# Pinning every weight fetch of a decoder block to the program's order on its queue

## The chip, the cores and the metric

The kernel runs on one core of one Trainium2 chip. The metric is the time of one execution on the device, in microseconds (us). The core has five engines that run side by side: TensorE (PE in the profile; PEld is its weight load), VectorE (DVE), ScalarE (ACT), GpSimd (POOL) and SyncE (SP). Here SP does nothing but issue transfers from HBM into the on-chip memory SBUF. It takes its instructions strictly one after the other: an issue whose buffer isn't free yet holds up all issues behind it.

## The reference

One decoder block of width 2048 over 256 tokens, all in float32. Cut to what matters here:

```python
def reference(x, mix_norm_w, w_in, ..., w_out, ffn_norm_w, w_gate_up, w_down, final_norm_w):
    h = x
    h = h + hybrid_mixer(rmsnorm(h, mix_norm_w), w_in, ..., w_out)
    h = h + swiglu(rmsnorm(h, ffn_norm_w), w_gate_up, w_down)
    return rmsnorm(h, final_norm_w)

def hybrid_mixer(h, w_in, ..., w_out):
    proj = einsum('bsd,de->bse', h, w_in)
    (q, k, v, g_out, gk_low, gate_b, gate_c, xc, merge_a, merge_b) = split(proj)
    y_a = rmsnorm(gla_chunked(q, k, v, log_g)) * silu(g_out)
    y_b = gate_b * causal_depthwise_conv(gate_c * xc, conv_w)
    merged = sigmoid(merge_a) * y_a + sigmoid(merge_b) * y_b
    return einsum('bse,ed->bsd', merged, w_out)

def swiglu(h, w_gate_up, w_down):
    gate, up = split(einsum('bsd,df->bsf', h, w_gate_up))
    return einsum('bsf,fd->bsd', silu(gate) * up, w_down)
```

Nearly all the work is the four large products with `w_in`, `w_out`, `w_gate_up` and `w_down`, and all of their weights are read from HBM once.

## The kernel before, in words

**Pieces.** The host lays every weight matrix out in pieces of 128 x 1024 floats, 512 KB each: two blocks of 128 rows by 512 columns (for k and q four by 256, for the last two strips of `w_down` four by 256). A list written out ahead (`stream_list`, made of `piece_list`, `gates_list`, `hidden_list` and `down_list`) says in which order the pieces are multiplied: first k, q and v with the linear attention, then the gates of the mixer, `w_out`, the hidden layer of the feed-forward part mixed with `w_down`, and the rest of `w_down`.

**What happens to a piece.** SP fetches it into a tile `raw` (5 buffers). ACT rounds it into a tile `hi` (`high`, L238; 6 buffers), DVE takes the rest, `raw - hi`, into a tile `lo` (`low`, L243; 5 buffers). PE then does three products for each pair of blocks (`mm3`, L347 to L349: lo, hi, hi), for plain pieces ("eights") for both halves of the tokens, 12 matmuls in all.

**Block sums.** Twelve pairs of 512-column strips (the four gc/xc pairs of the gates, as `GATES` names them, and eight fg/fu pairs of the hidden layer) are multiplied by a scheme with seven block products in place of eight (`sevens`, L398). For each of four quarters q of the depth it uses the pieces "11", "t1", "t3", "t2", "t4" and for the lower blocks "21" and "22" (`seven_list`, L100). Each has 6 matmuls. The four "t" pieces are sums of weight blocks, made by DVE when the piece is loaded (`sum_of`, L245):

- "11" fetches its block into the tile `y` (1 buffer) and uses it as it is.
- "t1" fetches another block into the tile `x` (2 buffers) and writes `raw = y + x` (L259).
- "t3" fetches a third block into `raw` and adds it into `x` (L265); "t2" adds `y` into `x` (L265); "t4" fetches a fourth block into `raw` and adds it into `x` (L265). "t3", "t2" and "t4" are all rounded out of the same tile `x`.

So each quarter makes four fetches: y, x, raw, raw. The tile `y` comes free once "t2" is summed; the two tiles `x` take turns.

**Mixing.** `mixed` (L107) sets plain pieces between the pieces of a pair: at most one behind each "t" piece first, then behind "21" and "22" (in one gate pair, where `early` is set, behind "11" too). In the hidden layer a pair but the first (which `FIRST` spaces by itself) gets 15 or 16 plain pieces, which lie behind the "t" pieces, so that the last eight pieces of a pair, 21 and 22, follow each other with nothing between; this is called the tail of the pair below.

**The order of the fetches.** `take` (L335) loads pieces in the list's order, up to five ahead of the one in use, by `load_piece` (L268). Plain pieces are fetched at L295 in `load_piece`, all blocks for the sums at L232 in `fetch`. Both are issues on SP's queue. The program's order on that queue is the order in which these lines are run. The order in which the engine in fact gets them is fixed when the program is built, by a scheduler that puts an instruction forward when its inputs and buffers are ready sooner. `pin` (`tc.keep_in_program_order`, L187) binds one instruction behind the one that the program traced just before it on the same engine; it adds no wait and no instruction. In the kernel before, some DVE and ACT instructions are pinned, and no transfer is.

**Other transfers on SP.** The start's loads of x, half of the stores at the end, and one quarter of the second reading of x into the tile `h` (`read_h`, L1000 to L1007), which comes after the mixer, in the middle of `w_out`: it is run seven pieces behind the gates' last (L1009), and `h` lies in memory that the gates' work tiles held before. The other three quarters of it go through POOL's queue.

Of the kernel before, what the change touches and what calls it, by code (L numbers as in the profile page):

```python
# [184 lines left out]
def block_kernel(ctx, tc, x, xt, cols_in, gkw_in, gku_in, gnw, conv_w, finw, w_in, w_out, w_gu, w_dn, out):  # L185
    nc = tc.nc
    pin = tc.keep_in_program_order  # L187
    mats = {"w_in": w_in, "w_out": w_out, "w_gu": w_gu, "w_dn": w_dn}
# [40 lines left out]
    def fetch(key, k0, pool=wraw, tag="raw"):  # L229
        mat, j, n, w = index[(key, k0)]  # L230
        raw = pool.tile([P, n, w], F32, tag=tag, name=tag, bufs={"x": 2, "y": 1}.get(tag))
        nc.sync.dma_start(raw, mats[mat][j].rearrange("p (k c) -> p k c", c=w))  # L232
        return raw

    def high(raw, piece, a=0, b=None):
        hi, n = piece[0], piece[2]
        ks = slice(a, b or n)
        nc.scalar.copy(hi[:, ks, :], raw[:, ks, :])  # L238

    def low(raw, piece, a=0, b=None):  # L240
        hi, lo, n = piece
        ks = slice(a, b or n)
        nc.vector.tensor_tensor(out=lo[:, ks, :], in0=raw[:, ks, :], in1=hi[:, ks, :].bitcast(F32), op=ALU.subtract)  # L243

    def sum_of(pair, what, q):  # L245

        one, two = pair
        if what == "21":
            return fetch(one, 4 * q + 2)
        if what == "22":  # L250
            return fetch(two, 4 * q + 2)
        if what == "11":
            held["y"] = fetch(one, 4 * q, held["pool"], "y")
            return held["y"]
        y = held["y"]
        if what == "t1":
            held["x"] = fetch(two, 4 * q, held["pool"], "x")
            raw = wraw.tile([P, 2, 512], F32, tag="raw", name="raw")
            nc.vector.tensor_tensor(out=raw, in0=y, in1=held["x"], op=ALU.add)  # L259
            return raw  # L260
        x = held["x"]
        if halfway and halfway[-1][0] is x:
            finish_low()
        other = y if what == "t2" else fetch(two if what == "t3" else one, 4 * q + 2)
        nc.vector.tensor_tensor(out=x, in0=x, in1=other, op=ALU.add)  # L265
        return x

    def load_piece():  # L268


        i = count["loaded"]
        count["loaded"] += 1
        if i < len(stream):
            key, k0 = stream[i]
            if isinstance(k0, tuple):
                n, w = 2, 512
                raw = sum_of(key, *k0)
                step = n
            else:
                mat, j, n, w = index[(key, k0)]  # L280
                raw = wraw.tile([P, n, w], F32, tag="raw", name="raw")

                step = n // 2 if i < 2 else n
            piece = [whi.tile([P, n, w], F32R, tag="hi", name="hi"), None, n]
            if isinstance(k0, tuple):
                high(raw, piece)
                halfway.append((raw, piece, key, k0))
            else:
                if i < 2:
                    piece[1] = wlo.tile([P, n, w], F32R, tag="lo", name="lo")  # L290
                for a in range(0, n, step):
                    b = a + step
                    if (i, a) in hooks:
                        hooks.pop((i, a))()
                    nc.sync.dma_start(  # L295
                        raw[:, a:b, :], mats[mat][j, :, a * w:b * w].rearrange("p (k c) -> p k c", c=w))
                    high(raw, piece, a, b)
                    if i < 2:
                        low(raw, piece, a, b)
                if i < 2:  # L300
                    ready[(key, k0)] = piece
                else:
                    halfway.append((raw, piece, key, k0))
        if len(halfway) > 1 or (halfway and i >= len(stream)):
            finish_low()

    def finish_low():
        raw, piece, key, k0 = halfway.pop(0)
        piece[1] = wlo.tile([P, piece[2], PIECE // piece[2]], F32R, tag="lo", name="lo")
        low(raw, piece)  # L310
        ready[(key, k0)] = piece
# [23 lines left out]
    def take(key, k0):  # L335
        while count["loaded"] <= len(stream) and count["loaded"] <= count["used"] + LOOK:
            load_piece()
        return ready.pop((key, k0))
# [902 lines left out]
```

## Time and profile before

| what | value |
|---|---|
| median of 3 runs | 1505.6 us (1505.35, 1505.6, 2092.2) |
| the profiled execution's own time | 1504.81 us |
| its span, first to last instruction | 1503.1 us |
| TensorE clock granted | 0.999 |
| ACT busy | 864.1 us, 57% |
| read from HBM | 351.03 MB |
| transfers, mean over the span | 239 GB/s, the fastest fortieth 349 GB/s |
| weight fetches issued by SP | 650: 362 at L295, 288 at L232 (192 into raw, 48 into x, 48 into y) |

The page counts the time that an engine is busy and, ahead of each group of instructions, the time that it sat idle and what ended that. For a transfer it gives the time of issue on SP's queue and the time from there to landing. A step of the kernel is late only if PE has to wait for it, so the rows to look at are PE's waits; everything ahead of PE has some lead over it.

### The profile page before, as it was taken

The numbers are of one execution on the slowest core, as the hardware profiler recorded it, in microseconds if no ns is written. First come the engines' busy times: TensorE is split into PE (matmuls) and PEld (weight loads), VectorE is DVE, ScalarE is ACT, GpSimd is POOL, SyncE is SP. The second block draws the span as 40 slices with busy tenths as digits, with TensorE's granted clock in tenths as the row PEclk, the third lists the DMA queues.
The fourth block names the chain that finished last, engine by engine and source line by source line (L and its number), as shares of the span: only waits on it lengthen the run. The fifth ranks groups of instructions, "written<-read, shape, count | busy, mean of one in ns | idle before, by whom it ended". The sixth has DMA issues, their size and how long they took to land.

```text
span 1503.1 us, 19370 instructions
## 1 busy us (share of the span) xinstructions
PE 1489.7 (99%) x7064; PEld 1244.8 (83%) x7064; DVE 1277.8 (85%) x1283; ACT 864.1 (57%) x977; POOL 38.0 (3%) x60
## 2 busy tenths in 40 slices
PE   9999999999999999999999999999999999999997
PEld 8989988888887888888888888888888788888887
DVE  6785868979979878966689999999999999999975
ACT  7773546655655655654566755655565556565553
POOL 0030000000000000000000000000000000000000
PEclk9999999999999999999999999999999999999999
DMA  9656557876876878787677777776877788787782
GB/s 349 201 172 174 177 166 251 288 225 234 285 259 232 297 237 257 249 258 215 209 221 219 238 253 251 250 253 218 275 242 239 259 255 277 242 264 234 231 297 90
DMA packets 100128, 358.58 MB, mean 239 GB/s; under 512 B 11492, under 2 KB 11620, under 8 KB 99904
## 3 DMA queue, kind: packets, MB, share of 16 engines
q1 hardware_dynamic: 96656, 346.73, 70.8%
q0 software_dynamic: 2800, 8.89, 2.2%
q10 hardware_dynamic: 576, 1.72, 0.3%
q8 instruction: 55, 0.90, 0.2%
q14 instruction: 41, 0.34, 0.1%
HBM read 351.03 MB, written 2.10 MB: 235 GB/s over the span
## 4 chain that ended last, share of the span: by engine, by line
PE 53%; DVE 1%; issue 0%; ACT 0%; DVEq 0%; ACTq 0%
PE fg L347 8%; PE fg L349 8%; PE fg L348 8%; PE dn L347 5%; PE dn L349 5%; PE dn L348 5%; PE wo L347 2%; PE wo L348 2%; PE wo L349 2%; PE fu L349 1%; PE fu L347 1%; PE fu L348 1%; PE trb L595 1%; PE mb L349 0%; PE mb L348 0%
## 5 line engine op out<-in xcount | busy, mean ns | idle before, releaser
L243 DVE TENSOR_TENSOR lo<-raw,hi 128x1024 fp32r<-128x1024 f32 (+1 forms) x506 | 612.0, 1217 | 110.9 <-ACT hi L238 27.9
L238 ACT CAST hi<-raw 128x1024 fp32r<-128x1024 f32 (+1 forms) x506 | 523.9, 1047 | 269.9 <-PE gb L349 27.7
L238 ACT CAST hi<-x 128x1024 fp32r<-128x1024 f32 x144 | 151.7, 1053 | 267.4 <-DVE x L265 207.1
L243 DVE TENSOR_TENSOR lo<-x,hi 128x1024 fp32r<-128x1024 f32 x144 | 176.1, 1223 | 37.5 <-ACT hi L238 26.6
L347 PE MATMUL dn<-lo,acth 128*128 128x512 f32 (+1 forms) x368 | 140.7, 382 | 1.7 <-DVE h L1098 0.9
L349 PE MATMUL dn<-hi,acth 128*128 128x512 f32 (+1 forms) x368 | 139.9, 380 | 0.0
L348 PE MATMUL dn<-hi,actl 128*128 128x512 f32 (+1 forms) x368 | 139.9, 380 | 0.0
L265 DVE TENSOR_TENSOR x<-x,raw 128x1024 f32<-128x1024 f32 x96 | 117.0, 1218 | 12.0 <-DMA raw<-in_w_in_dram 7.7
L347 PE MATMUL fg<-lo,hh 128*128 128x512 f32 x288 | 112.4, 390 | 0.0
L349 PE MATMUL fg<-hi,hh 128*128 128x512 f32 x288 | 112.2, 390 | 0.0
L348 PE MATMUL fg<-hi,hl 128*128 128x512 f32 x288 | 112.2, 389 | 0.0
L347 PE MATMUL fg<-lo,sh 128*128 128x512 f32 x256 | 101.0, 395 | 0.0
L348 PE MATMUL fg<-hi,sl 128*128 128x512 f32 x256 | 99.9, 390 | 0.0
L349 PE MATMUL fg<-hi,sh 128*128 128x512 f32 x256 | 99.8, 390 | 0.0
L347 PEld LDWEIGHTS dn<-lo,acth 128*128 128x128 f32 x368 | 69.2, 188 | 15.8 <-DVE h L1098 1.8
L349 PEld LDWEIGHTS dn<-hi,acth 128*128 128x128 f32 x368 | 69.2, 188 | 13.3
L348 PEld LDWEIGHTS dn<-hi,actl 128*128 128x128 f32 x368 | 69.2, 188 | 12.9
L347 PEld LDWEIGHTS fg<-lo,hh 128*128 128x128 f32 x288 | 54.1, 188 | 11.8 <-DVE lo L243 0.5
L349 PEld LDWEIGHTS fg<-hi,hh 128*128 128x128 f32 x288 | 54.1, 188 | 11.3
L348 PEld LDWEIGHTS fg<-hi,hl 128*128 128x128 f32 x288 | 54.1, 188 | 11.0
L243 DVE TENSOR_TENSOR lo<-y,hi 128x1024 fp32r<-128x1024 f32 x48 | 58.5, 1218 | 4.8 <-ACT hi L238 2.1
L259 DVE TENSOR_TENSOR raw<-y,x 128x1024 f32<-128x1024 f32 x48 | 58.5, 1219 | 4.2 <-DMA y<-in_w_in_dram 3.3
(247 smaller groups left out, 3070.1 us busy)
## 6 DMA issues: line engine op xcount, KB each, us to landing
raw<-in_w_in_dram SPq DMA_DIRECT2D x254, 512.0 KB, 4.5
raw<-in_w_gu_dram SPq DMA_DIRECT2D x176, 512.0 KB, 4.4
raw<-in_w_dn_dram SPq DMA_DIRECT2D x88, 512.0 KB, 4.5
x<-in_w_gu_dram SPq DMA_DIRECT2D x32, 512.0 KB, 4.8
y<-in_w_gu_dram SPq DMA_DIRECT2D x32, 512.0 KB, 3.9
raw<-in_w_out_dram SPq DMA_DIRECT2D x32, 512.0 KB, 4.3
y<-in_w_in_dram SPq DMA_DIRECT2D x16, 512.0 KB, 4.4
x<-in_w_in_dram SPq DMA_DIRECT2D x16, 512.0 KB, 4.8
```

What stands on the lines that cost most here:

```text
L238: nc.scalar.copy(hi[:, ks, :], raw[:, ks, :])
L243: nc.vector.tensor_tensor(out=lo[:, ks, :], in0=raw[:, ks, :], in1=hi[:, ks, :].bitcast(F32), op=ALU.subtract)
L259: nc.vector.tensor_tensor(out=raw, in0=y, in1=held["x"], op=ALU.add)
L265: nc.vector.tensor_tensor(out=x, in0=x, in1=other, op=ALU.add)
L347: nc.tensor.matmul(ps, lhsT=sh, rhs=ml, start=first, stop=False, skip_group_check=onto)
L348: nc.tensor.matmul(ps, lhsT=sl, rhs=mh, start=False, stop=False, skip_group_check=onto)
L349: nc.tensor.matmul(ps, lhsT=sh, rhs=mh, start=False, stop=last, skip_group_check=onto)
L595: nc.tensor.transpose(out=ps[:, j, :], in_=src[:, j * P:(j + 1) * P], identity=ident)
```

## The change

Both lines that fetch weights wrap their issue in `pin`. Nothing else is changed: the same transfers, the same buffers, the same lists.

```diff
     def fetch(key, k0, pool=wraw, tag="raw"):
         mat, j, n, w = index[(key, k0)]
         raw = pool.tile([P, n, w], F32, tag=tag, name=tag, bufs={"x": 2, "y": 1}.get(tag))
-        nc.sync.dma_start(raw, mats[mat][j].rearrange("p (k c) -> p k c", c=w))
+        pin(nc.sync.dma_start(raw, mats[mat][j].rearrange("p (k c) -> p k c", c=w)))
         return raw
...
                     if (i, a) in hooks:
                         hooks.pop((i, a))()
-                    nc.sync.dma_start(
-                        raw[:, a:b, :], mats[mat][j, :, a * w:b * w].rearrange("p (k c) -> p k c", c=w))
+                    pin(nc.sync.dma_start(
+                        raw[:, a:b, :], mats[mat][j, :, a * w:b * w].rearrange("p (k c) -> p k c", c=w)))
                     high(raw, piece, a, b)
```

Each weight fetch is thereby bound behind whatever the program traced on SP just before it, a weight fetch or one of the other transfers.

## The prediction, made before the changed kernel ran

> **What bounds the kernel now.** I read the page's first lines, then the waits of TensorE (PE), then windows.
>
> ```profile
> span 1503.1 us, 19370 instructions
> PE 1489.7 (99%) x7064; PEld 1244.8 (83%) x7064; DVE 1277.8 (85%) x1283; ACT 864.1 (57%) x977; POOL 38.0 (3%) x60
> ```
>
> PE is busy for 1489.7 of 1503.1 us. All that it waited for, added up over the whole run, is this (us in total, times, longest):
>
> ```profile
> PE warm_ps L518 <- DVE spare L514: 1.3, 1, 1.3
> PE dn L347 <- DVE h L1098: 0.9, 2, 0.5
> PE trb L595 <- DVE sb L908: 0.9, 1, 0.9
> PE dn L347 <- DVE lo L243: 0.8, 1, 0.8
> PE g L347 <- DVE lo L243: 0.7, 1, 0.7
> PE gc L347 <- DVE lo L243: 0.5, 1, 0.5
> PE gb L347 <- DVE ya L919: 0.2, 1, 0.2
> PE k L348 <- DVE lo L243: 0.2, 1, 0.2
> ```
>
> The first and the last of these belong to the start, which the change leaves alone. The other six make 4.0 us, and only three of them, 0.8 + 0.7 + 0.5 = 2.0 us, are waits for a weight piece that came late. So PE sets the time, and no order of the fetches can win more than these few us. What it can do is to lose: in the hidden layer DVE is nearly as full as PE. The next windows are a stretch of the gates with about two pairs and two single pairs of the hidden layer (columns: length, busy time of PE, PEld, DVE, ACT, POOL, clock, share of the DMA engines, GB/s).
>
> ```profile
> 400.00:640.00 240.00, 238.39 (x1058) 196.51 (x1057) 211.62 (x197) 138.02 (x143) 9.94 (x18) 1.00 0.79 257
> 860.00:942.00 82.00, 82.00 (x371) 67.94 (x370) 76.50 (x73) 49.63 (x54) 0.00 (x0) 1.00 0.76 246
> 1109.00:1190.00 81.00, 80.51 (x359) 66.16 (x358) 76.32 (x73) 45.33 (x48) 0.00 (x0) 1.00 0.77 253
> ```
>
> In the last window DVE has 81.0 - 76.3 = 4.7 us to spare in one pair, in the gates 240.0 - 211.6 = 28.4 in two. That is the cover for anything that the change makes late on DVE.
>
> One rule speaks against the bound. The Trainium skill, Perfetto Trace Analysis, section Identifying the Most-Contended Engine, says that the busy share of matmuls is no measure of the distance to the limit, and that the busy share of the weight loads is. By it, 83% here, 1503.1 - 1244.8 = 258 us would be in hand. The window from 860 to 942 us disagrees: PE waits for nothing in it, 82.00 of 82.00, and the weight loads are at 67.94, 83%, so 83% is what full pace looks like in this kernel.
>
> **What the change moves.** It adds no instruction, no transfer and no wait. It only forbids the order that the issues have now. This is SP's queue around one pair, from the tail of the pair before (1080 us) to the third quarter of the next:
>
> ```profile
> 1080.54 0.42 SPq L232 DMA_DIRECT2D x<-in_w_gu_dram  x1
> ...
> 1083.63 2.75 SPq L232 DMA_DIRECT2D raw<-in_w_gu_dram  x2
> 1087.19 0.33 SPq L232 DMA_DIRECT2D y<-in_w_gu_dram  x1
> 1090.72 1.47 SPq L232 DMA_DIRECT2D raw<-in_w_gu_dram  x2
> 1094.26 0.33 SPq L232 DMA_DIRECT2D x<-in_w_gu_dram  x1
> 1095.39 6.16 SPq L232 DMA_DIRECT2D raw<-in_w_gu_dram  x4
> ...
> 1119.94 0.33 SPq L232 DMA_DIRECT2D y<-in_w_gu_dram  x1
> ...
> 1132.57 0.42 SPq L232 DMA_DIRECT2D x<-in_w_gu_dram  x1
> 1136.88 0.33 SPq L232 DMA_DIRECT2D y<-in_w_gu_dram  x1
> ```
>
> The code has y, then x, in each quarter ("11" stands just ahead of "t1"). The trace has them otherwise: the first two x and the first y of the pair are fetched between the eight raw fetches of the tail before, and the third x goes out ahead of its y. The raw fetches among themselves are already in the code's order. So the change moves addends, x nearly always and y at the start of a pair, to a later place. There are 12 pairs, each with one start and three inner quarters.
>
> *Inner quarters.* y goes out when it does now, since its one buffer comes free with the sum of "t2", and x follows at once behind it. What that costs is how much later than y the x lands. The start of the first pair, the one place with y and x back to back in the code's order, tells it; then come the landings in the hidden layer (y first, then x) and the three sums of the pair above:
>
> ```profile
> L232 SPq DMA_DIRECT2D y<-in_w_in_dram x1: 327/327/327, 212.1 to 212.1; - x1
> DMA to landing us min/median/max: 3.6/3.6/3.6
> ...
> L232 SPq DMA_DIRECT2D x<-in_w_in_dram x2: 425/428/432, 212.5 to 212.9; - x2
> DMA to landing us min/median/max: 4.5/5.3/6.0
> ```
>
> ```profile
> DMA to landing us min/median/max: 3.3/3.9/5.0
> ...
> DMA to landing us min/median/max: 4.2/5.9/7.0
> ```
>
> ```profile
> 1108.73 1.22 DVE L259 TENSOR_TENSOR raw<-y,x 128x1024 f32<-128x1024 f32 x1
> 1125.27 1.21 DVE L259 TENSOR_TENSOR raw<-y,x 128x1024 f32<-128x1024 f32 x1
> 1141.46 1.22 DVE L259 TENSOR_TENSOR raw<-y,x 128x1024 f32<-128x1024 f32 x1
> ```
>
> At the start y lands at 212.1 + 3.6 = 215.7 and the first x at 212.5 + 4.5 = 217.0, 1.3 us behind it. Second quarter: y, issued at 1119.9, lands by the median at 1123.8, x would at 1125.1, and the sum begins at 1125.27: nothing lost. Third: y at 1136.9 + 3.9 = 1140.8, x at 1142.1, the sum begins at 1141.46: 0.6 us late. The fourth I take like the third. That makes 1.2 us per pair on DVE. The early x bought little, as its landing shows: 5.9 us in the middle against 3.9 for y, since it was put behind a queue that was already full.
>
> PE sees this only where it has no lead left. In most pairs the 4.7 us swallow the 1.2; in the three places where PE already waits for a piece I let all of it through: 3 x 1.2 = **+3.6 us**. Bounds: 0, if the lead holds everywhere, and 12 x 1.2 = 14.4, if it holds nowhere.
>
> *The tails.* Three transfers leave the tail of each pair, where raw lands slowly (issues between 1095 and 1102 us):
>
> ```profile
> DMA to landing us min/median/max: 4.1/4.9/5.7
> ```
>
> The fastest landing in the hidden layer is 3.3 and one transfer displaces the next by 1.3, so the pieces there can come about 1 us sooner, which is enough to end the three waits for late pieces: **-2.0 us**. Bounds: 0, and -4.0, if all six waits go.
>
> *The starts of pairs.* y and x are now issued behind the tail's last raw, at the earliest at 1095.39 + 6.16 = 1101.6. y lands by 1106.6 (5.0, the slowest), x 1.3 later at 1107.9, and the sum begins at 1108.73. I cost it at **0**; the raw fetches ahead hide it, 0.8 us remain, and with the slowest x (7.0) it would be 1102.0 + 7.0 - 1108.7 = 0.3 us, 3 us in 12 pairs.
>
> *The reading of h.* SP's share of it is traced ahead of the 13th and 14th pieces of `w_out` (counted in the lists), and stands behind them now, because it waits for the last transposes of the mixer:
>
> ```profile
> 717.62 7.89 SPq L295 DMA_DIRECT2D raw<-in_w_out_dram  x4
> 730.73 0.38 SPq L1007 DMA_DIRECT2D h<-in_x_dram  x1
> ...
> SPq L1007 <- PE trb L595: 4.9, 1, 4.9
> ...
> L295 SPq DMA_DIRECT2D raw<-in_w_out_dram x2: 328/328/328, 722.5 to 725.2; - x2
> ...
> DMA to landing us min/median/max: 4.9/7.3/9.3
> ...
> 700.00:748.00 48.00, 33.95 (x145) 26.78 (x146) 1.38 (x2) 1.00 0.67 215
> ```
>
> Pinned, both wait for h: they go out at 731.1 and 731.5 in place of 722.5 and 725.2, up to 8.6 us later. The last row counts matmuls into wo: 145 have begun by 748.0, so the 13th piece (12 a piece) begins there. With the slowest landing of h, 9.3, and the rounding and rest of 1.05 and 1.22 us
>
> ```profile
> L238 ACT CAST hi<-x 128x1024 fp32r<-128x1024 f32 x144 | 151.7, 1053 | 267.4 <-DVE x L265 207.1
> L243 DVE TENSOR_TENSOR lo<-x,hi 128x1024 fp32r<-128x1024 f32 x144 | 176.1, 1223 | 37.5 <-ACT hi L238 26.6
> ```
>
> it is ready at 742.7. The lead on PE hides it with 5.3 us over: **0**. Behind them queue the first pair's y and x, now fetched far ahead; without the cover the place costs at most 8.6 - 5.3 = 3.3 us.
>
> **The sum.** 1504.8 (the profiled execution's own time; its span and 1.7 around it) + 3.6 - 2.0 = 1506.4. The median of the runs lies 0.8 above the profiled execution: **1507.2 us**.
>
> **Rivals.**
>
> *The tails win.* All lateness is swallowed and the six waits vanish: 1505.6 - 4.0 = 1501.6. For it: the spare 4.7 us per pair. Against it: half of these waits are for work (L1098, L908, L919) that has no weight in it.
>
> *Nothing that PE sees.* The issues change places, or hardly do, and PE's waits stay as they are: 1505.6. The rows of the queue speak against the second, the lead of PE for the first.
>
> *The lateness adds up.* The lead is used up in every pair: 1505.6 + 14.4 = 1520.0. For it: three places have no lead now. Against it: 1.2 is a quarter of 4.7.
>
> *Slower: the addend becomes DVE's clock.* If x, behind y in a full queue, takes as long as the slowest now does, 7.0 against 3.9, each inner quarter is 3.1 us late and DVE stands still in front of the sum, since all its later work is behind it. Three make 9.3 us per pair; 4.7 are covered, 4.6 go through. The gates' pairs have 14 us of room each; the first hidden pair, mixed with `w_out`, I count with them. Seven pairs make 32.2, 1537.8 us. It decides from 4.7 / 3 = 1.6 us per quarter on. Against it: the back-to-back landing, 1.3. The Trainium skill, Trainium Kernel Development and Optimization, section Best Practices, asks for two buffers so that transfers overlap with compute; x has two and would use the second later than now. By that advice this rival has it; the rows say that the second buffer's head start was mostly spent in the queue.
>
> *PE was not at its limit.* If the rule on weight loads held, a smoother supply could free up to 258 us, but nothing in this change touches the spacing of the matmuls, and without waits they stand as close as anywhere.
>
> **How the numbers follow.** Forecast 1507.2: 0.47. Nothing seen, 1505.6: 0.15. Tails win, 1501.6: 0.17. Lateness adds up, 1520.0: 0.14. Addend as clock, 1537.8: 0.06. PE not at its limit: 0.01. The range runs from 1501.4 to 1520.5, which leaves out the last two and the edges. 2% of 1505.6, 30.1 us, is about what a measurement of this kernel can tell from no change. Faster by that is only the last case, as PE's busy time alone, 1489.7, is above 1475.5: 0.01. Slower by that is the fourth rival: 0.06. The rest is within: 0.93.
>
> **What would show it.** In the queue's timeline y stands directly ahead of x in every quarter, and no x or y stands in a tail. x lands 1 to 2 us behind y, at a shorter time from issue than 5.9. DVE's waits for an addend at L259 come to some 12 x 1.2 = 14 us in all. PE's waits for lo stay under 6 us. h stands ahead of two more raw fetches of `w_out`, and PE has no wait there. I am wrong if PE's waits for lo repeat once per quarter or per pair, if PE waits near 748 us, or if the time falls under 1501.

## The result, and the profile after

The changed kernel takes 1523.2 us in the median of five runs (1520.2 to 1524.7), against 1505.6 us for the kernel before: 1.0110 times as long, 95% interval 1.0093 to 1.0128. (The ratio is that of the means, without the one slow execution of the kernel before, 2092.2 us.) By the medians that is 17.6 us more, 2.7 us above the upper end of the predicted range and 16.0 above the predicted time. The profiled execution took 1523.48 us, with a span 18.7 us longer than before.

First the page of the changed kernel, span and busy times:

```profile
span 1521.8 us, 19369 instructions
PE 1497.4 (98%) x7064; PEld 1245.5 (82%) x7064; DVE 1275.5 (84%) x1283; ACT 859.8 (56%) x977; POOL 38.0 (2%) x60
```

The work is the same; PE's busy time grew by 7.7 us (1497.4 against 1489.7), so part of the loss isn't a wait at all. PE's waits in the changed kernel (us in total, times, longest):

```profile
PE trb L595 <- DVE sg L1057: 4.6, 4, 2.0
PE fg L347 <- DVE lo L243: 3.6, 7, 0.9
PE tr L581 <- ACT hraw L584: 2.6, 1, 2.6
PE dn L347 <- DVE h L1098: 1.9, 2, 1.2
PE g L347 <- DVE lo L243: 1.4, 1, 1.4
PE warm_ps L518 <- DVE spare L514: 1.3, 1, 1.3
PE trb L595 <- issue: 0.5, 1, 0.5
PE gc L347 <- DVE lo L243: 0.5, 1, 0.5
PE k L348 <- DVE lo L243: 0.2, 1, 0.2
```

Without the start they come to 15.1 us; before they were 4.0. Waits for a late weight piece (lo) are the smaller part, 5.5 us. The larger part is for *finished work*: the transposes of a finished hidden block (`trb`, of the product `sg`) and of the normalised h (`tr`). No fetch feeds those. How a late fetch holds them up is the core of this case.

DVE's waits for an addend at L259, and the queue of SP around a tail and an inner quarter of the changed kernel:

```profile
DVE raw L259 <- DMA x<-in_w_gu_dram: 16.6, 20, 3.0
DVE raw L259 <- DMA x<-in_w_in_dram: 7.4, 4, 3.0
```

```profile
1127.93 0.33 SPq L232 DMA_DIRECT2D y<-in_w_gu_dram  x1
1128.31 0.42 SPq L232 DMA_DIRECT2D x<-in_w_gu_dram  x1
...
1176.52 16.12 SPq L232 DMA_DIRECT2D raw<-in_w_gu_dram  x8
1192.69 0.43 SPq L232 DMA_DIRECT2D y<-in_w_gu_dram  x1
1193.17 0.42 SPq L232 DMA_DIRECT2D x<-in_w_gu_dram  x1
```

The order is the one foretold: y directly ahead of x, and no addend among the eight raw fetches of the tail. The sums wait 24.0 us for x, where before it was 4.2, and nearly all of that for y. Taken row by row, 16.5 of the 24.0 us lie at inner quarters and 7.5 at starts of pairs.

**Where the time goes.** One row for each kernel splits the loss: DVE's product of a finished hidden block, with the start of its first and last instance (ns of one: min, median, max; then first and last start). Before, then after:

```profile
L1057 DVE SCALAR_TENSOR_TENSOR sg<-u,r,sg x16: 737/746/753, 857.7 to 1443.1; 128x512 f32<-128x512 f32 x16
```

```profile
L1057 DVE SCALAR_TENSOR_TENSOR sg<-u,r,sg x16: 741/752/753, 861.1 to 1461.9; 128x512 f32<-128x512 f32 x16
```

Up to the first one 3.4 us are lost (861.1 - 857.7). From there to the last the hidden layer takes 600.8 in place of 585.4 us: 15.4 us. These two numbers are read from the same row for every experiment below and called **the head** and **the hidden stretch**. They belong to the profiled execution, which lies up to 2.4 us from the median of its kernel. The gates lose nothing: SP's issue of h, which waits for the mixer's last transposes, stands at 730.00 us after and at 730.73 before. Their sums do wait for x (7.4 us), but the gates have the room.

### The profile page after: what moved, and what is told of

Its sections match the earlier page's. It is cut to its first block, busy times and chain, and to the rows that moved or that the text cites. A ratio compares the mean times of both kernels' runs of the same rounds, so it can differ in the third digit from the quotient of the medians.

```text
span 1521.8 us, 19369 instructions
## 1 busy us (share of the span) xinstructions
PE 1497.4 (98%) x7064; PEld 1245.5 (82%) x7064; DVE 1275.5 (84%) x1283; ACT 859.8 (56%) x977; POOL 38.0 (2%) x60
## 4 chain that ended last, share of the span: by engine, by line
PE 86%; DVE 6%; DMA 3%; issue 2%; ACT 2%; SPq 0%; DVEq 0%; ACTq 0%
PE fg L347 6%; PE fg L349 6%; PE fg L348 6%; PE dn L347 4%; PE dn L348 4%; PE dn L349 4%; DVE lo L243 3%; PE gc L347 3%; PE gc L348 3%; PE gc L349 3%; PE v L348 2%; PE v L347 2%; PE v L349 2%; PE gb L349 2%; PE gb L347 2%
## 5 line engine op out<-in xcount | busy, mean ns | idle before, releaser
L349 PEld LDWEIGHTS dn<-hi,acth 128*128 128x128 f32 x368 | 69.2, 188 | 13.4
L259 DVE TENSOR_TENSOR raw<-y,x 128x1024 f32<-128x1024 f32 x48 | 58.6, 1220 | 24.0 <-DMA x<-in_w_gu_dram 16.6
```

The costliest lines, as they stand in the source:

```text
L349: nc.tensor.matmul(ps, lhsT=sh, rhs=mh, start=False, stop=last, skip_group_check=onto)
```

## The experiments

Line numbers in an experiment's rows are those of its own kernel, up to eight lines further down. Each was timed beside the kernel before, in 4 to 11 executions; ratios are to that.

### Which of the pins does it

*The addends free*: plain fetches and h pinned, x and y not.

```diff
-        pin(nc.sync.dma_start(raw, mats[mat][j].rearrange("p (k c) -> p k c", c=w)))
+        load = nc.sync.dma_start(raw, mats[mat][j].rearrange("p (k c) -> p k c", c=w))
+        if tag not in ("x", "y"):
+            pin(load)
```

> The changed kernel with the addends x and y not pinned; all fetches into raw stay pinned, behind h too. Theory (the pins cost where they move the addends, and at h): only the loss at h is left, 1505.6 + 4.4 = 1510.0. Rival 1 (the addends are all of it): 1505.6. Rival 2 (the pins on raw, or the order that they give the other engines, cost by themselves): above 1514.

Measured: 1505.47 us, ratio 1.0005 (0.9996 to 1.0013); head +1.4, hidden stretch +0.5 (859.1 to 1445.0). That is the first rival's number, not the theory's: without the pins on the addends there is no loss, to within the interval's 2 us. The plain fetches pinned behind h, which stand behind it in this kernel's queue too, cost little by themselves, but not nothing: PE waits 1.5 us for `hraw` at 742 us, where it waited for nothing before, and the head is longer by about that.

*h on POOL's queue*, all weight fetches pinned:

```diff
-            (nc.gpsimd if j else nc.sync).dma_start(h[:, :, j * 512:(j + 1) * 512], xv[:, :, j * 512:(j + 1) * 512])
+            nc.gpsimd.dma_start(h[:, :, j * 512:(j + 1) * 512], xv[:, :, j * 512:(j + 1) * 512])
```

> The changed kernel with the one quarter of the reading of h that SP issues moved to POOL's queue, so that no weight fetch can stand behind it. Matched matmuls of the two traces lie 0.7 us apart just before 736 us (the changed one ahead) and 3.7 us the other way at 756 us. Theory (the reading of h holds up the 13th and 14th pieces of w_out, and PE stalls): 4.4 us come back, 1518.8 us, and no wait of PE between 735 and 760. Rival (the lead hides it, as predicted, and the loss there comes from the first pair's late addends): 1523.

Measured: 1519.63 us, ratio 1.0090 (1.0075 to 1.0105), near the theory's number. That is 3.6 us below the changed kernel by the medians, 3.0 by the ratios, whose intervals overlap; the head is +1.2 in place of +3.4. The rows at 740 us show what h on SP's queue does (ACT, then PE, of the changed kernel):

```profile
741.10 1.04 ACT L238 CAST hi<-y 128x1024 fp32r<-128x1024 f32 x1 [1.59 <-DMA y<-in_w_gu_dram]
742.05 0.84 ACT L584 ACTIVATE hraw<-tr,cols 128x256 f32<-128x256 f32 x2
```

```profile
742.93 0.66 PE L581 MATMUL tr<-ident,h 128*128 128x128 f32 x4 [2.62 <-ACT hraw L584]
```

y of the first pair is queued behind h and two raw fetches (issued at 731.41, h at 730.00) and lands at 741.1. In ACT's order its rounding stands ahead of `hraw`, which has all that it needs; PE waits for `hraw`. Before, the same order did no harm, as y was there:

```profile
739.04 1.05 ACT L238 CAST hi<-y 128x1024 fp32r<-128x1024 f32 x1
739.99 0.83 ACT L584 ACTIVATE hraw<-tr,cols 128x256 f32<-128x256 f32 x2
```

The late y isn't the whole of it, though. Wherever fetches of `w_out` are pinned behind h and y is rounded ahead of `hraw`, PE waits here, also where y is in time: 1.5 us with the addends free, 1.4 to 2.5 us in three kernels below (y free, starts early, both edits). There the rounding of a piece of `w_out` that was fetched behind h holds up `hraw` (rows under *Both edits together*). With h on POOL's queue the wait for `hraw` is 0.3 us.

*x free, y pinned*:

```diff
+        if tag not in ("x",):
+            pin(load)
```

> The changed kernel with only x not pinned: x goes out early everywhere, y stays at its place in the code, which is late at the starts of pairs and unchanged in the inner quarters. Theory (the starts of pairs cost the most, about 9 us in the hidden layer, because y and x are both fetched behind the tail, and y alone is enough to be late; the inner quarters about 4): 1519. Rival (x, which lands behind y, is what is waited for): 1505.6 + 4.4 = 1510.

Measured: 1517.10 us, ratio 1.0080 (1.0067 to 1.0093); head +4.2, hidden stretch +6.6. The theory was near, the rival not.

*y free, x pinned*:

```diff
+        if tag not in ("y",):
+            pin(load)
```

> The changed kernel with only y not pinned. x is bound behind its y, so at the starts of pairs both go out early, and in the inner quarters x follows y as in the changed kernel. Theory (starts about 9 us, inner quarters about 4, h 4.4): 1505.6 + 4.4 + 4 = 1514. Rival (the inner quarters, three per pair, cost the most, as the lateness of x predicted): 1519 and more.

Measured: 1516.71 us, ratio 1.0079 (1.0065 to 1.0093); head +3.7, hidden stretch +10.6; by its time between theory and rival. Each half of the pins does most of the harm: the parts don't add up to the whole (8.0 + 7.9 against 11.0 thousandths). With x free, x is early everywhere and only y comes late, at the starts of pairs. There the second mechanism can be seen at its plainest (waits of PE, then DVE):

```profile
PE trb L597 <- DVE sg L1059: 6.3, 5, 2.5
```

```profile
860.76 1.23 DVE L261 TENSOR_TENSOR raw<-y,x 128x1024 f32<-128x1024 f32 x1 [2.73 <-DMA y<-in_w_gu_dram]
861.91 0.75 DVE L1059 SCALAR_TENSOR_TENSOR sg<-u,r,sg 128x512 f32<-128x512 f32 x1
```

The build had put the next pair's sum ahead of the finished block's product on DVE. The sum waits 2.73 us for y, the product stands behind it, and PE waits for the product. In the kernel with both starts pinned (below) the build put that product, at 860.23, ahead of the sum, and PE doesn't wait there. So the price of one late y depends on what the build happened to put behind it.

### Starts and inner quarters

*x ahead of y.* All pinned; the code fetches x where it fetches y, just ahead of it:

```diff
         if what == "11":
+            held["x"] = fetch(two, 4 * q, held["pool"], "x")
             held["y"] = fetch(one, 4 * q, held["pool"], "y")
             return held["y"]
...
-            held["x"] = fetch(two, 4 * q, held["pool"], "x")
```

> All pins stay; the code fetches x just ahead of y in each quarter, not just behind it. So x goes out while y still waits for its buffer, in the inner quarters about as in the kernel before; the starts of pairs stay late. Theory (what counts is the place of an addend on the queue, and inner quarters and starts cost about as much, 12 us each by itself, 17 together): the inner quarters' share of the lateness goes, about 1517, and the waits of DVE for x at L259 fall from 24 us to under 8. Rival (x lands late because the engines are full, wherever it stands): no change, 1523.

Measured: 1509.04 us, ratio 1.0021 (1.0011 to 1.0031). Neither the theory nor the rival had this: one exchange wins back 14 of the 17.6 us, though the starts are as late as in the changed kernel. The sums no longer wait for x at all; they wait 18.2 us for y in place of 24.0 for x, half of it at starts.

*Starts early.* All pinned, y ahead of x; the next pair's first y and x are fetched ahead of the tail's eight raw:

```diff
+    pairs = [key for key, k0 in stream if k0 == ("11", 0)]
...
         if what == "21":
+            if q == 0 and pair != pairs[-1]:
+                later_one, later_two = pairs[pairs.index(pair) + 1]
+                held["y"] = fetch(later_one, 0, held["pool"], "y")
+                held["x"] = fetch(later_two, 0, held["pool"], "x")
             return fetch(one, 4 * q + 2)
...
-            held["y"] = fetch(one, 4 * q, held["pool"], "y")
+            if q or pair == pairs[0]:
+                held["y"] = fetch(one, 4 * q, held["pool"], "y")
...
-            held["x"] = fetch(two, 4 * q, held["pool"], "x")
+            if q or pair == pairs[0]:
+                held["x"] = fetch(two, 4 * q, held["pool"], "x")
```

> All pins stay; the code fetches the next pair's first y and x ahead of the eight tail pieces of the pair before, so that the starts of pairs are early, by hand. Inner quarters as in the changed kernel, x behind y. Theory (the place on the queue alone sets it): as with y not pinned, 1517, and no wait at 740. Rival (it is the pin that costs, by the order that the other engines get when the program is built): 1520 and more.

Measured: 1515.62 us, ratio 1.0063 (1.0050 to 1.0076), near what was expected in time, but PE does wait at 742.5 us (1.4 us for `hraw`), where no wait was expected; hidden stretch +8.9. *Both edits together* (the fetch ahead of the tail with x first, and in each later quarter):

```diff
+                held["x"] = fetch(later_two, 0, held["pool"], "x")
+                held["y"] = fetch(later_one, 0, held["pool"], "y")
...
+            if q or pair == pairs[0]:
+                held["x"] = fetch(two, 4 * q, held["pool"], "x")
+                held["y"] = fetch(one, 4 * q, held["pool"], "y")
```

> All pins stay; both edits together: x ahead of y in each quarter, and the first x and y of the next pair ahead of the tail. Theory (place on the queue): all of the loss comes back, 1505 plus or minus 2. A gain over the kernel before is possible, since the tails carry only the addends that stand ahead of them: down to 1502. Rival (pins cost by themselves): above 1510.

Measured: 1507.73 us, ratio 1.0017 (1.0008 to 1.0026), 0.7 us above what was expected; hidden stretch -0.6 (859.6 to 1444.4), head +1.9. The head comes from PE's wait at h, with a y that nobody waits for (ACT, then PE):

```profile
739.06 1.05 ACT L239 CAST hi<-raw 128x1024 fp32r<-128x1024 f32 x1 [1.46 <-DMA raw<-in_w_out_dram]
...
740.64 1.03 ACT L239 CAST hi<-y 128x1024 fp32r<-128x1024 f32 x1
741.57 0.83 ACT L590 ACTIVATE hraw<-tr,cols 128x256 f32<-128x256 f32 x2
```

```profile
742.46 0.66 PE L587 MATMUL tr<-ident,h 128*128 128x128 f32 x4 [2.48 <-ACT hraw L590]
```

*Both, and h on POOL's queue*:

```diff
+            nc.gpsimd.dma_start(h[:, :, j * 512:(j + 1) * 512], xv[:, :, j * 512:(j + 1) * 512])
```

> As the run with both edits, and all four quarters of h on POOL's queue, so that nothing but weights stands on SP there. Theory: with the first hidden pair's addends early, h costs nothing or under 2 us; 0 to 2 us below the run with both edits. Rival (h holds up the queue whenever it is ahead of weights): 4 us below it.

Measured: 1505.95 us, ratio 1.0002 (0.9993 to 1.0011): as expected, and the time of before. With every fetch pinned, then, the old time comes back when the order written is a good one and h is off this queue; no version beat it.

*Only the starts pinned*, the inner quarters' x and y free:

```diff
+        if tag == "raw" or k0 == 0:
+            pin(load)
```

> Only the first y and the first x of each pair are pinned, with the plain fetches and h; the other three quarters' addends go out when the build wants them, so early again. It tells the price of the late starts alone. Theory: with the addends of the inner quarters early, the lead grows back inside each pair and the late starts cost what the kernel with x ahead of y lost, 3 to 5 us: 1508 to 1510 us. Rival: a late y at a start does its harm by itself, as in the run with only x unpinned, where y was late at the starts and the time was 1517.1: 1515 to 1518 us.

Measured: 1509.83 us, ratio 1.0028 (1.0019 to 1.0037), the theory's number. *The exchange at the starts only*:

```diff
+            if q == 0:
+                held["x"] = fetch(two, 4 * q, held["pool"], "x")
             held["y"] = fetch(one, 4 * q, held["pool"], "y")
...
+            if q:
+                held["x"] = fetch(two, 4 * q, held["pool"], "x")
```

> Everything pinned as in the changed kernel, but at the start of each pair x is fetched ahead of y (the inner quarters keep y, x). Theory: the 14 us that the full exchange won back come from the inner quarters, where x no longer lands 1.3 us behind y; at the starts the exchange only moves the conversion of y behind the normalised h at 740 us: 2 to 4 us below the changed kernel, 1518 to 1520 us. Rival: the gain sits at the starts, where the wait of ScalarE for y moves behind the finished block: 1510 us, and the next run finds little.

Measured: 1520.99 us, ratio 1.0102 (1.0087 to 1.0116), 1 us above what the theory had. Its rounding of y on ACT stands behind `hraw`, and PE's wait for that is down to 0.4 us, but the hidden stretch stays at +13.4:

```profile
L1060 DVE SCALAR_TENSOR_TENSOR sg<-u,r,sg x16: 745/752/754, 859.2 to 1458.0; 128x512 f32<-128x512 f32 x16
```

*The exchange in the inner quarters only* (the same two conditions the other way round):

```diff
+            if q:
+                held["x"] = fetch(two, 4 * q, held["pool"], "x")
             held["y"] = fetch(one, 4 * q, held["pool"], "y")
...
+            if q == 0:
+                held["x"] = fetch(two, 4 * q, held["pool"], "x")
```

> Everything pinned, x ahead of y in the three inner quarters alone; the starts keep y, x. Theory: most of the 14 us come back, but the stall at 740 us stays: 1511 to 1514 us. Rival (gain at the starts): 1520 us or more.

Measured: 1511.91 us, ratio 1.0034 (1.0022 to 1.0047), as expected. The wait for `hraw` is there as in the changed kernel, and the hidden stretch is nearly back to normal, 587.9 us, +2.5:

```profile
PE tr L584 <- ACT hraw L587: 2.6, 1, 2.6
```

```profile
L1060 DVE SCALAR_TENSOR_TENSOR sg<-u,r,sg x16: 743/750/754, 860.7 to 1448.6; 128x512 f32<-128x512 f32 x16
```

Set out by the order at the starts and in the inner quarters (ratio to before, with the intervals given above):

| starts of pairs | inner: y, x | inner: x, y | inner: free |
|---|---|---|---|
| late, y then x | 1.0110 (the change) | 1.0034 | 1.0028 |
| late, x then y | 1.0102 | 1.0021 | |
| ahead of the tail | 1.0063 | 1.0017 | |
| free | | | 1.0005 |

Across a row, y ahead of x in the inner quarters costs 7.6, 8.1 and 4.6 thousandths: 11.4, 12.2 and 6.9 us. Down the second column the late starts cost 0.4 to 1.7 thousandths, 0.6 to 2.6 us (the 0.4 isn't clear of the noise); down the first, where the inner quarters are late too, 3.9 to 4.7 thousandths, 5.9 to 7.1 us. The two together cost 3.0 and 3.5 thousandths more than the sum of the two apart; the intervals of four ratios together leave about 2.5 to either side. That they feed on the same lead is the likely reading; no run shows it by itself.

The waits agree over all kernels. In the seven pairs of the hidden stretch DVE stands still ahead of the inner quarters' sums (`raw<-y,x`, added up row by row) for 6.4 to 8.6 us in each of the six kernels in which x goes out behind y on SP's queue in the inner quarters, and their hidden stretch is 8.9 to 20.8 us longer than before. In all others it is 0.0 to 2.6 us, and the stretch -0.6 to +6.6.

### Why y ahead of x is dear and x ahead of y is cheap

y has one buffer, x two. In the kernel with x first, x goes out at 1133.85, as soon as a raw's turn allows, and y at 1138.17, when its buffer is free; in the changed kernel both wait for y's buffer and leave at 1144.70 and 1145.08. To see whether it is this queueing, *x was moved to POOL's queue*, with the code's order, y then x, and all pins kept:

```diff
-        pin(nc.sync.dma_start(raw, mats[mat][j].rearrange("p (k c) -> p k c", c=w)))
+        queue = nc.gpsimd if tag == "x" else nc.sync
+        pin(queue.dma_start(raw, mats[mat][j].rearrange("p (k c) -> p k c", c=w)))
```

> The changed kernel, all fetches pinned on their queue and the code's order kept (y, then x), but x goes out on GpSimd's queue instead of SP's, where the program has next to nothing else. Theory (x is late in the inner quarters because, on one queue, it stands behind y, and y's issue waits for its single buffer; x's own two buffers are free long before): x goes out several us ahead of y, the waits of the sum for x in the inner quarters vanish, and what is left is the price of the late y at the starts and near the normalised h, so about the time of the run with only the starts pinned: 1508 to 1512 us. Rival (the price is in how the build arranges the other engines around a y that is written ahead of x, or in the transfers' own order on the DMA engines, not in the queue): 1518 us or more.

Measured: 1528.10 us, ratio 1.0151 (1.0137 to 1.0165). By its time the theory misses widely and the rival has it, and the kernel is the slowest but one. The rows split it:

```profile
L1058 DVE SCALAR_TENSOR_TENSOR sg<-u,r,sg x16: 741/748/753, 876.3 to 1465.6; 128x512 f32<-128x512 f32 x16
```

The hidden stretch is 589.3 us, +3.9 where the changed kernel has +15.4, and in the window from 1000 to 1500 us DVE has no wait for x left (the changed kernel has 7.4 us in 12 waits there). That is what the queueing theory says. The loss is the head, +18.6, and lies in the gates, some 12 us, and at h, some 5 (PE's waits of the whole run, then POOL's queue):

```profile
PE gc L348 <- DVE lo L244: 3.8, 7, 1.3
PE g L348 <- DVE lo L244: 3.3, 3, 1.7
PE tr L582 <- ACT hraw L585: 3.2, 1, 3.2
```

```profile
331.30 0.56 POOL L890 DMA_DIRECT2D u<-u  x1 [60.29 <-DVE u L955]
...
333.88 0.52 POOL L895 DMA_DIRECT2D u<-u  x1
334.40 0.56 POOL L233 DMA_DIRECT2D x<-in_w_in_dram  x1
```

I had taken POOL's queue for next to empty. In the gates it carries the convolution's shifts; there the pinned x stands behind six of these, the first of which waits on DVE, and lands 9.3 us after its issue. It is the same trap on another queue. At 744.6 us x stands behind three quarters of h and lands only 13.9 us later, but PE's wait at h isn't for that: it is the changed kernel's, with y on SP's queue (ACT waits 1.60 us for y at 753.54). The hidden stretch supports the theory; x goes out early at the starts of its pairs too, so this run alone doesn't part inner quarters from starts. The run with only the inner quarters exchanged does, and agrees.

*The rounding of y one piece later.* To move ACT's rounding of y behind finished work without touching the fetches:

```diff
             if isinstance(k0, tuple):
-                high(raw, piece)
+                if k0[0] != "11":
+                    high(raw, piece)
                 halfway.append((raw, piece, key, k0))
...
         piece[1] = wlo.tile([P, piece[2], PIECE // piece[2]], F32R, tag="lo", name="lo")
+        if isinstance(k0, tuple) and k0[0] == "11":
+            high(raw, piece)
         low(raw, piece)
```

> The changed kernel with the fetches as they are, but the rounding of each y on ScalarE is written one piece later, so that at the starts of pairs it stands behind the normalised h and the finished block's silu in the order of that engine. Theory (a late addend does its harm by standing ahead of a finished block's work on an in-order engine): the wait of TensorE for the normalised h, 2.6 us, and the half-clock behind it go, and the waits of the transposes of sg shrink from 4.6 us; the late sums of the inner quarters stay: 4 to 8 us below the changed kernel, 1515 to 1519 us. Rival (the order on ScalarE plays no part, only the landing of the addends does): 1522 to 1524 us.

Measured: 1534.56 us, ratio 1.0199 (1.0178 to 1.0220). A miss, and a poor test: the edit makes y's own rest late in all 48 quarters, since its rounding now comes behind that of the sum, and y's piece is the first of a quarter that PE needs.

```profile
PE fg L350 <- DVE lo L243: 6.0, 9, 1.9
...
PE tr L584 <- ACT hraw L587: 0.3, 1, 0.3
```

Its one clean point is the last row: with the order on ACT turned round, the wait for `hraw` falls from 2.6 to 0.3 us.

## Why the prediction was wrong, by its own steps

**What bounds the kernel, and the order of the queue: right.** PE sets the time, nothing could be won, and SP's queue came out as foretold. So did the landing: the page gives a median of 4.8 us for x and 3.8 for y, x issued 0.4 later, so 1.4 us behind y; 1.3 was predicted.

**Inner quarters, +3.6: the cover was wrong, and this is the step that failed most.** The lateness came out about as predicted: 1.2 us per pair, 14.4 in all, against 16.5 measured at the inner sums, and 8.6 in the seven pairs of the hidden stretch, 1.2 each. (The other 7.5 of the 24.0 us are the starts.) The single waits spread widely; the longest in the hidden stretch is here, where x took 6.7 us and the sum stood still for 2.49 (DVE, changed kernel):

```profile
1148.14 1.22 DVE L265 TENSOR_TENSOR x<-x,raw 128x1024 f32<-128x1024 f32 x1
1151.85 1.22 DVE L259 TENSOR_TENSOR raw<-y,x 128x1024 f32<-128x1024 f32 x1 [2.49 <-DMA x<-in_w_gu_dram]
1152.99 1.22 DVE L243 TENSOR_TENSOR lo<-x,hi 128x1024 fp32r<-128x1024 f32 x1
```

What failed is "In most pairs the 4.7 us swallow the 1.2", and with it the price of three places only. The 4.7 us are DVE's idle time summed over a pair, and they don't lie where the sum waits. The rows show why: behind the waiting sum stands `lo<-x`, the rest of the *piece before*, "t4", which needs nothing of that sum. Right behind it, at 1154.27, PE has one of its seven waits for a piece of `fg` (0.80 us); they lie in three of the eight hidden pairs. An in-order engine turns the lateness of one input into lateness of all that is queued behind, and spare time further on can't be spent backwards. I had written this very thing under the rival "addend becomes DVE's clock", "since all its later work is behind it", and left it out of the forecast. In place of 3.6 us the inner order cost 7 to 12: in the hidden layer about all of the lateness came through, in the gates none.

**The starts, 0: wrong in combination.** y was to go out at 1101.6 at the earliest and land within 5.0 us. In the changed kernel, where the same matmuls run 5.7 us later at this place, it went out at 1108.5, 1.2 later than that, and took 6.3 us behind the eight raw of the tail; x, issued at 1109.0, took 7.1. The sum began at 1116.8, 2.4 us late, with other work of DVE drawn ahead of it. At all starts together the sums stood still for 7.5 us, where I had 0. With the lead intact the starts cost 1 to 3 us, about the bound I had given (3); with the lead gone, 6 to 7. What PE waits for is again finished work (ACT, DVE and PE at a start, changed kernel):

```profile
1197.68 1.05 ACT L238 CAST hi<-raw 128x1024 fp32r<-128x1024 f32 x1 [1.47 <-DMA raw<-in_w_gu_dram]
1198.64 0.72 ACT L1054 ACTIVATE sg<-v,r 128x512 f32<-128x512 f32 x1
```

```profile
1199.39 0.75 DVE L1057 SCALAR_TENSOR_TENSOR sg<-u,r,sg 128x512 f32<-128x512 f32 x1 [1.90 <-ACT sg L1054]
```

```profile
1200.19 0.66 PE L595 MATMUL trb<-ident,sg 128*128 128x128 f32 x4 [1.96 <-DVE sg L1057]
```

The silu of the finished block stands behind the rounding of a tail piece for which ACT waits 1.47 us, then the product, then PE's transposes. No addend stands in these rows: this piece was fetched when a buffer came free, and SP's waits in the tail are for DVE (12.0 us for `lo`). The Trainium skill, PSUM — Partial Sum Buffer, section Engine vs sequencer instructions, says that the queues of ScalarE, VectorE and GpSimd are strictly first in, first out; the rows of ACT and DVE here, the two at 741.10 and 742.05 and POOL's agree.

**The reading of h, 0: wrong, and I looked at the wrong piece.** PE has no wait for a piece of `w_out`, as I had worked out. But the rounding of these pieces stands on ACT ahead of `hraw` too, and costs PE 1.4 to 2.5 us where y is in time (addends free, y free, starts early, both edits). And "Behind them queue the first pair's y and x, now fetched far ahead" was the sentence to follow up: y lands 9.7 us after its issue and its rounding holds `hraw` for 1.59 us; together the two hold PE for 2.62. I had asked what waits for the moved fetch, not what is *queued behind* what waits for it. I had named a wait of PE near 748 us as a sign of being wrong; it came at 740 to 743.

**The tails, -2.0: didn't come.** The raw fetches of a tail do land sooner: the eight of the tail at 1176 us took 4.3 us in the median, those of the same tail before 4.8.

```profile
DMA to landing us min/median/max: 3.4/4.3/5.3
```

```profile
DMA to landing us min/median/max: 4.5/4.8/5.6
```

But PE's waits for lo went from 2.0 to 5.5 us: a shorter way from issue to landing didn't end these waits. That what counts there is when buffers and engines are free is my reading, not shown.

**Not in the sum at all: the clock.** After the two longest standstills PE ran at half clock (windows of the changed kernel; the third number from the end is the granted clock, 0.50):

```profile
743.80:747.20 3.40, 3.40 (x10) 2.61 (x9) 3.40 (x5) 2.68 (x4) 0.00 (x0) 0.50 1.03 410
1201.20:1204.60 3.40, 3.40 (x10) 2.66 (x9) 3.40 (x5) 0.28 (x1) 0.00 (x0) 0.50 0.65 175
```

Twice 3.4 us at half clock are 3.4 us lost, which the profile books as busy time of PE (of the 7.7 us by which that grew). Of the other 4.3 some 2.2 are a matter of booking, by an estimate: the last matmul ahead of a wait is booked with its full 0.39 us, others with the 0.23 us to the next start, and there are 14 more such waits. The rest I can't place. So the wait for `hraw` costs 2.6 + 1.7 = 4.3 us.

**The rivals.** "The lateness adds up", 1520.0, came nearest, by its reason in part and in part by luck: that the lead is used up holds in the hidden layer, where the seven pairs of the hidden stretch were late by 1.2 us each, but not in the four pairs of the gates, which lose nothing; the starts, h and the clock, which it didn't have, make up for that. "The addend becomes DVE's clock" named the right mechanism and over-priced it (1537.8). It leaned on the advice to use two buffers (the Trainium skill, Trainium Kernel Development and Optimization, section Best Practices); the exchange of x and y bears the advice out and sharpens it: sending x out early, which its second buffer allows, is worth 7 to 12 us here, but only if x's issue doesn't stand behind an issue that waits for a single buffer.

**What stays open.** Every edit of the fetches also made the build arrange PE, ACT and DVE anew (the product at 860 us ahead of the sum in one kernel, behind it in another). How many of the 7 to 12 us are the late x itself, and how many this arrangement, no run parted; that waits and loss go together over all kernels speaks for the late x. Nor does any run explain why x free and y pinned (1.0080) costs more than only the starts pinned (1.0028), beyond the two places shown: head +4.2 against +2.5, and hidden stretch +6.6 against +3.4.

## What to carry to other kernels

In an in-order queue, put the issue whose buffer is free first and the one that must wait last; a pin on the written order is only as good as that order. When an input comes later, ask on each engine that waits for it what is queued behind the waiting instruction: here it was finished blocks, which no fetch feeds and on which PE waits at once. Spare time averaged over a stage is no cover; only the lead at the very place is, and two small delays don't simply add: late starts and late inner quarters cost more together than apart, the two halves of the pins less.

## What the runs showed of the hardware

**A short standstill can halve the clock; what counts is the idle share of a fixed window.** Over all profiled kernels here, PE stood still for more than 2 us between two matmuls twelve times (from start to start, less the usual 0.23 us; 2.07 to 3.40 us). Eight of these were followed by 3.4 us at a granted clock of 0.5, four were not, among them one of 2.88 us. One of 1.89 us was, with a second of 0.58 us close by; no shorter one was.

The traces tell what decides. In each, all changes of the clock lie whole multiples of 3.413 us apart: the two slow stretches of the changed kernel begin 457.4 us apart, 134 times that. With the time cut into these windows, each of the nine stretches of half clock ahead of a kernel's end follows a window in which PE was idle for 57% or more, each such window is followed by one, and none with 56% or less is. The two nearest to the limit (length, busy time of PE; changed kernel, then x on POOL's queue):

```profile
1197.78:1201.19 3.41, 1.45 (x10) 0.95 (x9) 1.80 (x2) 2.81 (x4) 0.00 (x0) 1.00 0.91 356
1201.19:1204.60 3.41, 3.41 (x10) 2.67 (x9) 3.41 (x5) 0.28 (x1) 0.00 (x0) 0.50 0.65 174
```

```profile
875.27:878.68 3.41, 1.51 (x9) 1.36 (x10) 3.41 (x4) 1.73 (x3) 0.00 (x0) 1.00 0.33 136
878.68:882.09 3.41, 3.41 (x17) 2.81 (x16) 3.41 (x5) 2.36 (x3) 0.00 (x0) 1.00 0.76 221
```

The standstill of 2.88 us did no harm because a window's border cut it in two: PE was busy for 1.67 us of the one window and 2.43 of the other.

The Trainium skill, TensorE: Matmul & The Clock Gate, section What's actually happening, has the clock halved after at least one idle window of about 3.4 us, with windows that run freely. The length of the windows, and that the same standstill sometimes does and sometimes doesn't, agree with that. That the window must be idle as a whole doesn't: 1.96 of 3.41 us were enough, at 1197.8 us of the changed kernel.
